# Taking hi and lo in one matmul in more weight pairs, with the MLP pairs in another order and a convolution tap on ScalarE

## The chip, the cores and the metric

The kernel runs on one core of one Trainium2 chip. The metric is the device time of one execution in microseconds; the times given are medians of several runs. The profile is of one execution, recorded by the hardware.

## The reference

One layer of a streaming encoder, sequence 512, width 1024, float32 throughout. Cut to what matters:

```python
h = rmsnorm(x, norm_mix_g)
u, v, bg, cg, xs, ga, gb = split(h @ w_in)             # seven times 1024 columns
u, v = gelu(u), rmsnorm(gelu(v), norm_v_g)
a = spatial_gating(u, v, w_s, b_s)                     # branch A
c = bg * causal_dwconv3(cg * xs, conv_w)               # branch B
m = sigmoid(ga + b) * (a @ w_proj_a) + sigmoid(gb + b) * (c @ w_proj_b)
x = x + m @ w_out
z = relu(rmsnorm(x, norm_ff_g) @ w_ff1)                # 1024 -> 4096
x = x + (z * z) @ w_ff2                                # 4096 -> 1024
return rmsnorm(x, norm_final_g)
```

`causal_dwconv3` is a convolution over time with three taps per channel.

## The kernel before, in words

Activations lie transposed: 128 channels on the partitions, 512 positions along the row. Every float32 operand is split in two fp32r parts, hi (a rounded copy, made by ScalarE, L117) and lo (what is left, a subtraction by VectorE, L118), and a product is taken as hi·hi + hi·lo + lo·hi.

Weights come in two kinds. A **unit** is one column of 128 outputs: 8 steps of depth with three matmuls of 512 columns each (`unit_k`, L265 to L267), 24 in all; two units arrive in one load of 1 MB. A **pair** is two such columns done by a fast block scheme with seven products instead of eight (P1, P2, E, P6, F, P7, D), again one load of 1 MB. For a pair VectorE also forms sums of the weight blocks (`add1`, L218; `add2`, L222 and L223); its four operands a1, s31, s42 and a22 are then split into hi and lo. Each product has four steps of depth on 256 positions. In the **narrow** form (`block_pair`, `product` with L295 to L297) each step is three matmuls of 256 columns: hi·hi, hi·lo, lo·hi, all summed in the same 256 columns of a PSUM bank. In the **wide** form (`wide_pair`, L290 and L292) the moving operand holds hi and lo side by side, so one matmul of 512 columns makes hi·hi in one half of the bank and hi·lo in the other, and one of 256 columns adds lo·hi to the first half. The two halves must then be added when the bank is emptied: ScalarE copies (L345, L351, L353, L363, L370), VectorE adds (L347, L356, L364) and folds the halves (L342, L371). The narrow form empties with half as wide copies (L311, L316, L318, L326) and additions (L313, L321, L327). P7 and D of a pair are put off (`late`): they run inside the next pair or the next unit.

Before the change the eight gate pairs are wide; the four pairs of stream c, the four of stream xs, and the sixteen of the MLP are narrow.

Operands are prepared ahead. The plan (`plan_units`, `plan_pair`) lists all loads, sums and splits in the order of use, and each unit's half and each product takes one step of it (`pump`), if one of four weight buffers is free (a22 has one of its own). A raw load is issued two loads ahead, when the splits of the load two before it have been issued, into one of two raw buffers. Work tiles of 512 (`temp`, L107) come from a pool of eight. A scheduler then lays the instructions of each engine out in its order.

Branch B (`c_pair`, four times): a pair of c, a pair of xs, two units; c is multiplied by R squared (L656, L660, L661), the product of both streams passes three taps (`conv`, first tap L668, the others L670) and a product with R (L671), and is multiplied by the units' results (L695).

The MLP: 16 pairs make 32 tiles of z (`ff1_pair`; relu times the norm's factor at L771, L776 and L777, the square at L767, the split at L117 and L118), in four chunks of eight tiles; after the pairs of a chunk come eight units of w_ff2 with that chunk's tiles, added to the result (L912). Pairs run one ahead of the chunk: 5 pairs, 8 units, 4 pairs, 8 units, 4 pairs, 8 units, 3 pairs, the last units. The z tiles lie in ten slots used in turn.

Of the kernel before, what the change touches and what calls it, by code (L numbers as in the profile page):

```python
# [9 lines left out]
F32R = mybir.dt.float32r  # L10
BF16 = mybir.dt.bfloat16
AF = mybir.ActivationFunctionType
ALU = mybir.AluOpType

P = 128
S = 512
D = 1024
KT = D // P
KS = KT // 2
NB = S // P  # L20
N2 = S // 2
HALF = 512
FT = 32
NCH = 4
CF = FT // NCH
NP1 = FT // 2
EPS = 1e-6
N_WARM = 10
N_SLOTS = 32
N_WBUF = 4  # L30


V_BGATE, V_GV, V_CONV, V_GFF, V_GFIN, V_GMIX, V_N = 0, 16, 24, 48, 56, 64, 72
# [3 lines left out]
def hybrid_block(ctx, tc, xT, vecs, w_v, w_main, w_pair, w_s, b_s, out_a, out_b):  # L37
# [12 lines left out]
    nc = tc.nc  # L50
# [46 lines left out]
    def slots(n, name, dtype=F32):  # L97
        return [Slot(f"{name}{k}", dtype) for k in range(n)]
# [8 lines left out]
    def temp(name, n=S):  # L107
        t = work.tile([P, S + 2], F32, tag="temp", name=name)
        return t[:, :n]

    def col(base, j):
        return vec[:, base + j : base + j + 1]
# [12 lines left out]
    def bank():  # L125
        return ps.tile([P, S], F32, name="bank")
# [7 lines left out]
    loads = []  # L134
    wfree = list(range(N_WBUF))
    a22_busy = [False]
# [34 lines left out]
    def add_step(fn):  # L171
        steps.append((fn, None))
# [24 lines left out]
    def plan_units(n):  # L197
        for _ in range(n // 2):
            ld = len(loads)
            loads.append(("u", len(units)))  # L200
            for e in range(2):
                units.append(add_operand(lambda ld=ld, e=e: raw_of[ld][:, 2 * e : 2 * e + 2, :]))
            add_step(lambda ld=ld: load(ld + 2))
# [3 lines left out]
    def plan_pair():  # L207
        ld = len(loads)
        loads.append(("p", len(pairs)))

        def raw(a, b):
            return raw_of[ld][:, a:b, :]

        s31, s42 = sums_t[0].t, sums_t[1].t

        def add1():

            nc.vector.tensor_tensor(s31, raw(1, 3), raw(3, 4).broadcast_to([P, 2, S]), op=ALU.add)  # L218

        def add2():  # L220

            nc.vector.tensor_tensor(s42[:, 1, :], s31[:, 1, :], raw(1, 2)[:, 0, :], op=ALU.add)  # L222
            nc.vector.tensor_tensor(s42[:, 0, :], s42[:, 1, :], raw(0, 1)[:, 0, :], op=ALU.add)  # L223

        tl = {}
        tl["a1"] = add_operand(lambda: raw(0, 2))
        add_step(add1)
        tl["s31"] = add_operand(lambda: s31)
        add_step(add2)
        tl["s42"] = add_operand(lambda: s42)  # L230
        tl["a22"] = add_operand(lambda: raw(2, 3), n=1)
        add_step(lambda: load(ld + 2))
        pairs.append(tl)
# [4 lines left out]
    def run_late():  # L238
        if late:
            late.pop(0)()  # L240
# [60 lines left out]
    def block_pair(p, right, first, second):  # L301

        A, P2, E = (bank() for _ in range(3))
        A_, P2_, E_ = (b[:, :N2] for b in (A, P2, E))
        c1, c2 = temp("c1"), temp("c2")
        product(p, right, "P1", A, True)  # L310
        nc.scalar.copy(c1[:, :N2], A_)  # L311
        product(p, right, "P2", P2, True)
        nc.vector.tensor_add(c1[:, :N2], P2_, c1[:, :N2])  # L313
        run_late()
        product(p, right, "E", E, True)
        nc.scalar.copy(c2[:, N2:], E_)  # L316
        product(p, right, "P6", A, False)
        nc.scalar.copy(c1[:, N2:], A_)  # L318
        run_late()
        product(p, right, "F", E, False)  # L320
        nc.vector.tensor_add(c1[:, N2:], E_, c1[:, N2:])  # L321
        first(c1)

        def p7():
            product(p, right, "P7", A, False)
            nc.scalar.copy(c2[:, :N2], A_)  # L326
            nc.vector.tensor_add(c2[:, N2:], c2[:, :N2], c2[:, N2:])  # L327

        def dd():
            product(p, right, "D", A, False)  # L330
            second(A_, c2)

        late.extend([p7, dd])
# [97 lines left out]
            nc.vector.tensor_add(acc, acc, sq)  # L431


    sums_t = slots(2, "wsum")
    plan_units(KT)
    for _ in range(KS):
# [9 lines left out]
    plan_units(KT)  # L446
    n_win = len(pairs)
    for ck in range(NCH):
        for _ in range(CF // 2 + (ck == 0) - (ck == NCH - 1)):
            plan_pair()  # L450
        plan_units(KT)


    xin_s = slots(KS, "xin")
# [62 lines left out]
    for i in range(2 * KT):  # L517
        h, k = divmod(i, KT)
# [36 lines left out]
    R2 = small.tile([P, S], F32, name="R2")  # L555
# [39 lines left out]
    for j in range(KT):  # L595
# [8 lines left out]
    right_x = right_of(  # L604
        lambda sl: x_s[sl].t[:, :, :N2], x_s[KS:], xc1, xc2
    )
# [17 lines left out]
    def next_pair():  # L624
        pair_no["next"] += 1
        return pair_no["next"] - 1
# [25 lines left out]
    def c_pair(j0):  # L652
        tc_, ys = {}, {}

        def c_first(c1):
            nc.vector.tensor_mul(c1, c1, R2)  # L656
            tc_[0] = c1

        def c_second(n21, c2):
            nc.vector.tensor_mul(c2[:, :N2], n21, R2[:, :N2])  # L660
            nc.vector.tensor_mul(c2[:, N2:], c2[:, N2:], R2[:, N2:])  # L661
            tc_[1] = c2

        def conv(e, z):
            j = j0 + e
            y = temp("y")
            w = [col(V_CONV + 8 * i, j) for i in range(3)]
            nc.vector.tensor_scalar(y, z[:, 0:S], w[0], None, op0=ALU.mult)  # L668
            for i in (1, 2):
                nc.vector.scalar_tensor_tensor(y, z[:, i : S + i], w[i], y, op0=ALU.mult, op1=ALU.add)  # L670
            nc.vector.tensor_mul(y, y, R)  # L671
            ys[e] = y

        def x_first(c1):
            z = temp("z", S + 2)
            nc.vector.memset(z[:, 0:2], 0.0)
            nc.vector.tensor_mul(z[:, 2 : S + 2], tc_[0], c1)
            conv(0, z)

        def x_second(n21, c2):  # L680

            z = temp("z", S + 2)
            nc.vector.memset(z[:, 0:2], 0.0)
            nc.vector.tensor_mul(z[:, 2 : N2 + 2], n21, tc_[1][:, :N2])
            nc.vector.tensor_mul(z[:, N2 + 2 : S + 2], c2[:, N2:], tc_[1][:, N2:])
            conv(1, z)

        block_pair(next_pair(), right_x, c_first, c_second)
        block_pair(next_pair(), right_x, x_first, x_second)
        pbs = []  # L690
        for e in range(2):
            pbs.append(bank())
            unit_matmuls(pbs[e], xh, xl)
        for e in range(2):
            nc.vector.tensor_mul(ys[e], pbs[e], ys[e])  # L695
            split_into(ch[j0 + e], cl[j0 + e], ys[e])
# [13 lines left out]
    for p in range(KS):  # L710
        gate(next_pair(), 1, 2 * p, sgs.__setitem__)
        last = p == KS - 1
        for e in range(2):
            j = 2 * p + e
# [25 lines left out]
    right_f = right_of(f_b11, fb2, ft1, ft2)  # L740
    xg = {}
    for n in range(KT):
        j = n // 2 + KS * (n % 2)
# [13 lines left out]

    acc2 = None
    Rf = small.tile([P, S], F32, name="R")
    z_s = slots(CF + 2, "z", F32R)  # L760

    def z_tile(i):
        t = z_s[i % len(z_s)].t
        return t[:, 0, :], t[:, 1, :]

    def z_split(i, t):
        nc.scalar.activation(t, t, AF.Square)  # L767
        split_into(*z_tile(i), t)
# [2 lines left out]
        nc.vector.scalar_tensor_tensor(c1, c1, 0.0, Rf, op0=ALU.max, op1=ALU.mult)  # L771
        z_split(i, c1)

    def z_second(i, n21, c2):

        nc.vector.scalar_tensor_tensor(c2[:, :N2], n21, 0.0, Rf[:, :N2], op0=ALU.min, op1=ALU.mult)  # L776
        nc.vector.scalar_tensor_tensor(c2[:, N2:], c2[:, N2:], 0.0, Rf[:, N2:], op0=ALU.min, op1=ALU.mult)  # L777
        z_split(i, c2)
# [77 lines left out]
    def ff1_pair(p):  # L856
        def first(c1):
            if p == 0:
                wait_rf.append(lambda: z_first(0, c1))
            else:  # L860
                z_first(2 * p, c1)

        def second(n21, c2):
            z_second(2 * p + 1, n21, c2)

        block_pair(n_win + p, right_f, first, second)
        if p == 0:
            r2.append(rstd_of(acc))

            def p7_and_rf(p7=late.pop(0)):  # L870
                p7()
                nc.vector.tensor_copy(Rf, spread(r2[0]))
                wait_rf.pop()()
            late.insert(0, p7_and_rf)
# [17 lines left out]
            release(us[e])  # L892
        return dict(enumerate(pys))

    done = 0
    for ck in range(NCH):
        end = min((ck + 1) * CF // 2 + 1, NP1)
        for p in range(done, end):
            ff1_pair(p)
        done = end  # L900
        zh, zl = zip(*[z_tile(ck * CF + i) for i in range(CF)])
        last = ck == NCH - 1
        if last:
            acc2 = [acc[:, :256], acc[:, 256:]]
        pys = side_by_side(zh, zl) if last else {}
        for j in range(KT - 2 if last else KT):
            if j in pys:
                py = pys[j]
            else:
                py = bank()  # L910
                unit_matmuls(py, zh, zl)
            nc.vector.tensor_add(res[j], py, res[j])  # L912
            if last:
                for hf in range(2):
                    sum_squares(acc2[hf], res[j][:, hf * N2 : (hf + 1) * N2], j, n=N2)
                scale_g(j, slice(0, S))
        if last:
            give(*fb11, *fb2, *ft1, *ft2)
            last_tiles([KT - 2, KT - 1])
# [67 lines left out]
```

## Time and profile before

| | us |
|---|---|
| median of 3 runs | 787.3 (786.64 to 787.36) |
| the profiled execution | 786.65 |
| its span, first to last instruction | 784.9 |
| TensorE busy | 776.3 |
| VectorE busy | 584.5 |
| ScalarE busy | 373.6 |

The profile lists, for each engine, when its instructions ran. PE is TensorE's matmuls, PEld its weight loads, DVE is VectorE, ACT ScalarE, SP the queue that issues the loads. A matmul's recorded length runs past the start of the next one, so the pace of matmuls is read from start to start. VectorE's and ScalarE's records overlap a little in the same way when an engine does not wait.

### The profile page before, as it was taken

To read this page: it belongs to the slowest core of one execution; us is meant where nothing else is said; L and a number is where in the kernel's file an instruction comes from. 1 tells how busy PE (TensorE), PEld (TensorE's weight loads), DVE (VectorE), ACT (ScalarE), POOL (GpSimd) and SP (SyncE) were. 2 spreads that over 40 slices of the span, in tenths; PEclk is the share of its full clock that TensorE was granted. 3 is DMA by queue.
4 is the path that set the end of the run, shared out by engine and by line. 5 is a ranking of instruction groups with operands and counts; after the bars stand their busy time and mean duration, and the time that the engine had idled before them with its cause. 6 is when DMAs were issued, how large, how long until landed. Compare 5 with 4: busy or idle time off the path is not lost.

```text
span 784.9 us, 11159 instructions
## 1 busy us (share of the span) xinstructions
PE 776.3 (99%) x4574; PEld 689.4 (88%) x4574; DVE 584.5 (74%) x878; ACT 373.6 (48%) x556; POOL 6.3 (1%) x14
## 2 busy tenths in 40 slices
PE   9999999999999999999999999999999999999996
PEld 6888888889999998888888999889988999889886
DVE  7849787777889889877779997647855686557644
ACT  8625364444344354544556576315642465226421
POOL 0000000000000000000000000000000000000000
PEclk9999999999999999999999999999999999999999
DMA  9602113331332223332633034320353024311403
GB/s 337 218 38 92 69 55 108 108 108 55 112 123 89 108 75 142 108 107 102 220 108 107 1 109 144 125 107 1 109 193 129 1 98 171 108 55 54 161 1 108
DMA packets 21442, 83.59 MB, mean 106 GB/s; under 512 B 1936, under 2 KB 2960, under 8 KB 17296
## 3 DMA queue, kind: packets, MB, share of 16 engines
q1 hardware_dynamic: 20384, 81.27, 29.5%
q10 hardware_dynamic: 1008, 1.61, 0.6%
q8 instruction: 36, 0.59, 0.3%
q14 instruction: 14, 0.11, 0.0%
HBM read 80.78 MB, written 2.10 MB: 106 GB/s over the span
## 4 chain that ended last, share of the span: by engine, by line
PE 96%; DMA 1%; DVE 1%; ACT 1%; issue 0%; POOLq 0%; DVEq 0%
PE bank L265 17%; PE bank L266 17%; PE bank L267 17%; PE bank L297 10%; PE bank L296 10%; PE bank L295 10%; PE bank L290 7%; PE bank L530 6%; PE bank L292 3%; PE bank L581 1%; DMA raw<-w_pair 1%; DVE wlo L118 0%; DMA vec<-vecs 0%; PE bank L422 0%; ACT whi L117 0%
## 5 line engine op out<-in xcount | busy, mean ns | idle before, releaser
L117 ACT CAST whi<-raw 128x1024 fp32r<-128x1024 f32 (+1 forms) x136 | 129.0, 950 | 160.8 <-PE bank L266 111.0
L118 DVE TENSOR_TENSOR wlo<-raw,whi 128x1024 fp32r<-128x1024 f32 (+1 forms) x136 | 148.7, 1094 | 17.0 <-ACT whi L117 15.4
L265 PE MATMUL bank<-z,whi 128*128 128x512 f32 (+1 forms) x272 | 102.7, 378 | 0.0
L266 PE MATMUL bank<-z,whi 128*128 128x512 f32 (+1 forms) x272 | 102.5, 377 | 0.0
L267 PE MATMUL bank<-z,wlo 128*128 128x512 f32 (+1 forms) x272 | 102.4, 376 | 0.0
L117 ACT CAST whi<-wsum 128x1024 fp32r<-128x1024 f32 x64 | 67.2, 1050 | 69.5 <-PE bank L266 39.0
L118 DVE TENSOR_TENSOR wlo<-wsum,whi 128x1024 fp32r<-128x1024 f32 x64 | 78.1, 1220 | 11.1 <-ACT whi L117 10.9
L297 PE MATMUL bank<-ft,wlo 128*128 128x256 f32 x256 | 72.5, 283 | 0.6 <-DVE wlo L118 0.6
L295 PE MATMUL bank<-ft,whi 128*128 128x256 f32 x256 | 72.5, 283 | 0.0
L296 PE MATMUL bank<-ft,whi 128*128 128x256 f32 x256 | 72.4, 283 | 0.0
L912 DVE TENSOR_TENSOR res<-bank,res 128x512 f32<-128x512 f32 x30 | 20.7, 691 | 60.4 <-PE bank L267 60.4
L267 PEld LDWEIGHTS bank<-z,wlo 128*128 128x128 f32 x272 | 51.2, 188 | 9.4
L265 PEld LDWEIGHTS bank<-z,whi 128*128 128x128 f32 x272 | 51.2, 188 | 9.1
L266 PEld LDWEIGHTS bank<-z,whi 128*128 128x128 f32 x272 | 51.2, 188 | 8.9
L296 PE MATMUL bank<-fb,whi 128*128 128x256 f32 x192 | 54.4, 283 | 0.0
L295 PE MATMUL bank<-fb,whi 128*128 128x256 f32 x192 | 54.4, 283 | 0.0
L297 PE MATMUL bank<-fb,wlo 128*128 128x256 f32 x192 | 54.3, 283 | 0.0
L265 PE MATMUL bank<-x,whi 128*128 128x512 f32 x128 | 50.4, 394 | 0.0
L266 PE MATMUL bank<-x,whi 128*128 128x512 f32 x128 | 50.0, 390 | 0.0
L267 PE MATMUL bank<-x,wlo 128*128 128x512 f32 x128 | 49.8, 389 | 0.0
L297 PEld LDWEIGHTS bank<-ft,wlo 128*128 128x128 f32 x256 | 49.1, 192 | 0.8 <-DVE wlo L118 0.8
L295 PEld LDWEIGHTS bank<-ft,whi 128*128 128x128 f32 x256 | 49.1, 192 | 0.3
(174 smaller groups left out, 1755.4 us busy)
## 6 DMA issues: line engine op xcount, KB each, us to landing
raw<-w_main SPq DMA_DIRECT2D x36, 1024.0 KB, 5.0
raw<-w_pair SPq DMA_DIRECT2D x32, 1024.0 KB, 4.8
vraw<-w_v SPq DMA_DIRECT2D x16, 256.0 KB, 5.4
xin<-xT SPq DMA_DIRECT2D x8, 256.0 KB, 5.0
res<-xT SPq DMA_DIRECT2D x8, 256.0 KB, 4.1
out_a<-o SPq DMA_DIRECT2D x4, 256.0 KB, 2.3
wsT<-w_sT ACTq DMA_DIRECT2D x2, 256.0 KB, 4.7
bsb<-b_sb ACTq DMA_DIRECT2D x2, 256.0 KB, 6.6
```

The source lines that it names most:

```text
L117: nc.scalar.copy(hi, src)
L118: nc.vector.tensor_tensor(lo, src, hi.bitcast(F32), op=ALU.subtract)
L265: nc.tensor.matmul(psum, hi[:, c], act_hi[k][:, cols], start=k == 0, stop=False)
L266: nc.tensor.matmul(psum, hi[:, c], act_lo[k][:, cols], start=False, stop=False)
L267: nc.tensor.matmul(psum, lo[:, c], act_hi[k][:, cols], start=False, stop=k == KT - 1)
L290: nc.tensor.matmul(two, w_hi[sl], x2[sl], start=first and sl == 0, stop=False, **kw)
L292: nc.tensor.matmul(half, w_lo[sl], x2[sl][:, 0, :], start=False, stop=sl == KS - 1, **kw)
L295: nc.tensor.matmul(half, w_hi[sl], x2[sl][:, 0, :], start=first and sl == 0, stop=False, **kw)
L296: nc.tensor.matmul(half, w_hi[sl], x2[sl][:, 1, :], start=False, stop=False, **kw)
L297: nc.tensor.matmul(half, w_lo[sl], x2[sl][:, 0, :], start=False, stop=sl == KS - 1, **kw)
L530: nc.tensor.matmul(vbanks[h][b], xs[k][:, b * P : (b + 1) * P], ws, start=k == 0 and ws is vh and xs is xh, stop=k == KT - 1 and xs is xl,)
L912: nc.vector.tensor_add(res[j], py, res[j])
```

## The change

Eleven MLP pairs (all but the first five) and the four pairs of stream c take the wide form. The order of the MLP is now, in each chunk, first a group of pairs, then four units, then one pair, then four units: 5 pairs (narrow), 4 units, 1 pair, 4 units; 3 pairs, 4 units, 1 pair, 4 units; the same once more; 2 pairs and the last units. The plan of loads follows the same order. Tiles of z lie in twelve slots instead of ten. The first tap of the convolution is a scaled copy on ScalarE. `c_second` and `z_second` work on a whole row of 512 instead of two halves; for the narrow MLP pairs the old form is kept as `z_second_ps`.

```diff
+N_NARROW = 5
+    def ff1_parts(ck):
+        h = CF // 2
+        ends = [min(ck * h + h + e, NP1) for e in (1, 2)]
+        begin = min(ck * h + 2, NP1) if ck else 0
+        return [range(begin, ends[0]), range(ends[0], ends[1])]
 ...
     for ck in range(NCH):
-        for _ in range(CF // 2 + (ck == 0) - (ck == NCH - 1)):
-            plan_pair()
-        plan_units(KT)
+        for part in ff1_parts(ck):
+            for _ in part:
+                plan_pair()
+            plan_units(KT // 2)
 ...
-        def c_second(n21, c2):
-            nc.vector.tensor_mul(c2[:, :N2], n21, R2[:, :N2])
-            nc.vector.tensor_mul(c2[:, N2:], c2[:, N2:], R2[:, N2:])
+        def c_second(c2):
+            nc.vector.tensor_mul(c2, c2, R2)
             tc_[1] = c2
 ...
-            nc.vector.tensor_scalar(y, z[:, 0:S], w[0], None, op0=ALU.mult)
+            nc.scalar.activation(y, z[:, 0:S], AF.Copy, scale=w[0])
 ...
-        block_pair(next_pair(), right_x, c_first, c_second)
+        wide_pair(next_pair(), right_x, c_first, c_second)
         block_pair(next_pair(), right_x, x_first, x_second)
 ...
-    z_s = slots(CF + 2, "z", F32R)
+    z_s = slots(CF + 4, "z", F32R)
 ...
+    def z_second(i, c2):
+        nc.vector.scalar_tensor_tensor(c2, c2, 0.0, Rf, op0=ALU.min, op1=ALU.mult)
+        z_split(i, c2)
 ...
-        block_pair(n_win + p, right_f, first, second)
+        if p < N_NARROW:
+            block_pair(n_win + p, right_f, first, lambda n21, c2: z_second_ps(2 * p + 1, n21, c2))
+        else:
+            wide_pair(n_win + p, right_f, first, second)
 ...
     for ck in range(NCH):
-        end = min((ck + 1) * CF // 2 + 1, NP1)
-        for p in range(done, end):
+        parts = ff1_parts(ck)
+        for p in parts[0]:
             ff1_pair(p)
 ...
         for j in range(KT - 2 if last else KT):
+            if j == KT // 2:
+                for p in parts[1]:
+                    ff1_pair(p)
```

## Rows read from the trace of the kernel before

**Rows 1.** Busy us, share of the span and instructions of two engines, the page.
```profile
PE 776.3 (99%) x4574; PEld 689.4 (88%) x4574; DVE 584.5 (74%) x878; ACT 373.6 (48%) x556; POOL 6.3 (1%) x14
```
**Rows 2.** Waits of TensorE: waiter, releaser, us in total, times, longest.
```profile
PE bank L297 <- DVE wlo L118: 0.6, 1, 0.6
```
**Rows 3.** Chain that ended last, in time order: start us, length us, what.
```profile
548.51 6.52 DMA raw<-w_pair
```
**Rows 4.** Busy us by stretch: span, PE, PEld, DVE, ACT, POOL, clock, DMA share, GB/s.
```profile
185.67:309.10 123.43, 123.43 (x858) 115.66 (x857) 106.55 (x162) 52.48 (x79) 0.00 (x0) 1.00 0.27 95
436.00:484.80 48.80, 48.80 (x409) 48.77 (x409) 45.01 (x73) 33.53 (x56) 1.91 (x1) 1.00 0.20 66
532.20:572.00 39.80, 39.25 (x318) 38.59 (x317) 31.95 (x47) 23.86 (x41) 0.00 (x0) 1.00 0.20 65
```
**Rows 5.** Timeline of TensorE, narrow MLP products: start us, length us, instruction.
```profile
473.24 0.28 PE L295 MATMUL bank<-fb,whi 128*128 128x256 f32 x1
...
477.56 0.28 PE L295 MATMUL bank<-ft,whi 128*128 128x256 f32 x1
```
**Rows 6.** Timeline of TensorE, two wide products of a gate pair.
```profile
100.39 1.09 PE L290 MATMUL bank<-x,whi 128*128 128x512 f32 x4
101.32 0.63 PE L292 MATMUL bank<-x,wlo 128*128 128x256 f32 x4
101.79 1.09 PE L290 MATMUL bank<-xc,whi 128*128 128x512 f32 x4
```
**Rows 7.** Chain in time order, first product of two successive gate steps.
```profile
350.56 0.91 PE bank L290 x4
...
371.28 0.91 PE bank L290 x4
```
**Rows 8.** Timeline of VectorE: two steps of branch B, two MLP units.
```profile
203.23 0.49 DVE L668 TENSOR_SCALAR y<-z,vec 128x512 f32<-128x512 f32 x1
...
234.33 0.49 DVE L668 TENSOR_SCALAR y<-z,vec 128x512 f32<-128x512 f32 x1
...
515.11 0.69 DVE L912 TENSOR_TENSOR res<-bank,res 128x512 f32<-128x512 f32 x1 [3.36 <-PE bank L267]
...
520.55 0.69 DVE L912 TENSOR_TENSOR res<-bank,res 128x512 f32<-128x512 f32 x1 [3.35 <-PE bank L267]
```
**Rows 9.** Timeline of VectorE, back to back in the run of four pairs.
```profile
542.56 1.21 DVE L118 TENSOR_TENSOR wlo<-raw,whi 128x1024 fp32r<-128x1024 f32 x1
543.69 0.68 DVE L223 TENSOR_TENSOR wsum<-wsum,raw 128x512 f32<-128x512 f32 x1
544.29 0.41 DVE L327 TENSOR_TENSOR c<-c 128x256 f32<-128x256 f32 x1
544.62 1.22 DVE L118 TENSOR_TENSOR wlo<-wsum,whi 128x1024 fp32r<-128x1024 f32 x1
```
**Rows 10.** Instruction groups by shape: count, busy us, mean ns, idle before.
```profile
L347 DVE TENSOR_TENSOR t<-bank,t 128x512 f32<-128x512 f32 x8 | 5.5, 685 | 0.5 <-PE bank L292 0.5
L345 ACT COPY t<-bank 128x512 f32<-128x512 f32 x8 | 4.7, 586 | 4.2 <-PE bank L292 4.2
L668 DVE TENSOR_SCALAR y<-z,vec 128x512 f32<-128x512 f32 x8 | 3.9, 482 | 0.1
L748 ACT ACTIVATE xg<-res,vec 128x512 f32<-128x512 f32 x8 | 5.8, 722 | 1.9 <-DVE res L746 1.7
```
**Rows 11.** Timeline of VectorE, run of four: first and last of three waits, the fetch.
```profile
534.37 0.42 DVE L313 TENSOR_TENSOR c<-bank,c 128x256 f32<-128x256 f32 x1 [0.86 <-PE bank L297]
...
538.69 0.42 DVE L321 TENSOR_TENSOR c<-bank,c 128x256 f32<-128x256 f32 x1 [0.90 <-PE bank L297]
...
555.05 1.22 DVE L218 TENSOR_TENSOR wsum<-raw 128x1024 f32<-128x1024 f32 x1 [2.38 <-DMA raw<-w_pair]
```
**Rows 12.** Loads on SP's queue, the page: count, KB each, median us to landing.
```profile
raw<-w_main SPq DMA_DIRECT2D x36, 1024.0 KB, 5.0
```
**Rows 13.** Timeline, last MLP pair: VectorE's last lo part, TensorE's matmul that reads it.
```profile
735.65 0.69 DVE L118 TENSOR_TENSOR z<-c,z 128x512 fp32r<-128x512 f32 x1 [1.35 <-ACT z L117]
...
738.95 0.39 PE L265 MATMUL bank<-z,whi 128*128 128x512 f32 x1
```

More of the change, by code (lines that the diff above doesn't have):

```diff
@@ L772, in z_first, with z_second_ps @@
         z_split(i, c1)
-    def z_second(i, n21, c2):
+    def z_second(i, c2):
+        nc.vector.scalar_tensor_tensor(c2, c2, 0.0, Rf, op0=ALU.min, op1=ALU.mult)
+        z_split(i, c2)
+    def z_second_ps(i, n21, c2):
         nc.vector.scalar_tensor_tensor(c2[:, :N2], n21, 0.0, Rf[:, :N2], op0=ALU.min, op1=ALU.mult)
@@ L861, in first, with second @@
                 z_first(2 * p, c1)
-        def second(n21, c2):
-            z_second(2 * p + 1, n21, c2)
-        block_pair(n_win + p, right_f, first, second)
+        def second(c2):
+            z_second(2 * p + 1, c2)
+        if p < N_NARROW:
+            block_pair(n_win + p, right_f, first, lambda n21, c2: z_second_ps(2 * p + 1, n21, c2))
+        else:
+            wide_pair(n_win + p, right_f, first, second)
         if p == 0:
@@ L893, in side_by_side @@
         return dict(enumerate(pys))
-    done = 0
     for ck in range(NCH):
-        end = min((ck + 1) * CF // 2 + 1, NP1)
-        for p in range(done, end):
+        parts = ff1_parts(ck)
+        for p in parts[0]:
             ff1_pair(p)
-        done = end
         zh, zl = zip(*[z_tile(ck * CF + i) for i in range(CF)])
```

## The prediction, made before the change was run

> **What bounds the kernel now.** I read the busy times first: TensorE works in 776.3 of 784.9 us, one matmul per weight load [rows 1]. A busy TensorE proves little by itself, so the list of its waits came next: in the whole span it waited once for another engine in mid-kernel, 0.6 us for a lo operand of VectorE [rows 2]. The chain in order of time shows where: between 548 and 565 us, in the run of four MLP pairs of the second chunk, behind a transfer of a pair's weights of 6.52 us [rows 3]. Then the stretches: in branch B (185.67 to 309.10) VectorE is busy 106.55 of 123.43 us; in the run of the first five MLP pairs 45.01 of 48.80; in the run of four, 31.95 of 39.80 [rows 4]. So TensorE's pace sets the end, and VectorE is the next bound, with little room where narrow pairs stand back to back. The reader should keep both in mind: the change buys TensorE time with VectorE time.
>
> **What TensorE gains.** A narrow product is 12 matmuls of 256 columns, a wide one 4 of 512 and 4 of 256: the same 3072 columns. Three narrow products (36 matmuls) start at 473.24 and the next at 477.56: 4.32 / 3 = 1.44 us [rows 5]. Wide products of the gate pairs start at 100.39 and 101.79: 1.40 us, 0.93 for the four wide matmuls and 0.47 for the four half ones [rows 6]. So a product gives 0.04 us and a pair of seven 0.28. A second way checks it: a gate step (one wide pair, two units) repeats every 371.28 - 350.56 = 20.72 us [rows 7], a unit every 520.55 - 515.11 = 5.44 us, and a step of branch B (two narrow pairs, two units) every 234.33 - 203.23 = 31.10 us [rows 8]. That makes a wide pair 20.72 - 10.88 = 9.84 and a narrow one (31.10 - 10.88) / 2 = 10.11: 0.27 us. Pairs made wide: 11 of the MLP's 16 and the 4 of c, 15 in all: **15 x 0.28 = 4.2 us off**.
>
> The Trainium skill ("TensorE: Matmul & The Clock Gate", section "Wait — 56ns, not 53.3ns?") speaks against this: it has a matmul take its columns at 2.4 GHz plus about 2.5 ns, so that four matmuls fewer per product would give an estimated 0.01 us instead of 0.04, and 1 us in all instead of 4.2. The rows do not agree: 256 columns are spaced 0.12 us in the narrow product and 0.1175 in the wide one, 512 columns 0.2325.
>
> **What VectorE pays.** Back to back, its instructions are spaced 1.13 us (128x1024), 0.60 (128x512) and 0.33 (128x256), less than their recorded lengths [rows 9]. I count by these. Preparing a pair's weights: three 1024 differences, one 1024 sum, one 512 difference, two 512 sums: 4 x 1.13 + 3 x 0.60 = 6.3 us, unchanged. Narrow emptying: three 256 additions, 1.0. Wide emptying: three 512 additions and four of 256: 3.1. An addition of 512 that reads the accumulator (0.685 us recorded) is as long as one of 512 elsewhere, so the same spacings serve [rows 9, 10]. The MLP's own work on the two results: 2.5 narrow, 2.4 wide. So an MLP pair needs 9.8 us of VectorE narrow and **11.8 wide, against TensorE's 9.8**: each wide pair in a run loses 2 us of VectorE's lead.
>
> ScalarE gains four copies of 0.59 in place of four of half the width and one half copy, under 1.3 us more per pair; it is busy 23.86 of 39.80 us in the run of four [rows 4], so I cost it at nothing while it does not wait.
>
> **Branch B.** Per step the c pair adds 2.1 us to VectorE (the two R2 products become one). The first tap leaves it: 2 x 0.48 us recorded [rows 10], 0.8 by spacing. Net +1.3, and TensorE's step is 0.28 shorter. VectorE's idle time there is (123.43 - 106.55) / 4 = 4.2 us a step, so 2.6 us remain. Both taps cost ScalarE 0.72 each [rows 10] and it is busy only 52.48 of 123.43 us. The new wait (VectorE's second tap behind ScalarE's first) has queued behind it the pair's own last two taps and the lo differences of coming operands; these are several us early. I take nothing; the bounds are 0 and 0.7 us a step (one tap fully exposed), 2.9 in all.
>
> **The MLP order.** Before, runs of 5, 4, 4 and 3 pairs; after, 5 narrow, then 4 units, 1 wide, 4 units; twice 3 wide, 4 units, 1 wide, 4 units; 2 wide and the last units. A single pair sits among units where VectorE works about 1.7 of each 5.44 us: covered. The run of four with the 0.6 us stall is gone: **-0.6**. The question is the run of three. At its start the first pair's operands are ready and the second's sums too. By the time TensorE needs the third pair's s42 (16 products, 22.4 us later) VectorE must have done: emptying and results of the first pair 5.5, operands of the second 4.0, of the third up to s42 5.7, emptying of the second and the first piece of the third 4.9: 20.1 us. Before, three early waits for TensorE between 534 and 539 us took 2.27 us of such a run whatever the load [rows 11]. 20.1 + 2.3 = 22.4: just enough, nothing left. Then the first unit behind the run: its raw weights can be fetched only when the second pair's a22 is split, some 17 us into the run; the fetch takes 5.0 us as a median and 6.52 in the run of before [rows 3, 12]; copy and difference add 2.3 us. That is 24.3 to 25.8 against a need at 26.6. Each of the two runs may stall between 0 and 2.5 us (1.5 if the chain waits of the run of before come on top, 1.0 if the fetch meets a queue). I take 0.5, near the low end, since the sum just closes: **+1.0**. SP's queue holds the loads in the new order, two ahead as before; the single pair's load goes between two unit loads, each with more than 5 us to spare.
>
> **The end.** The last pair's second result passes one more ScalarE copy and one more addition, about 1 us. Before, its lo part started at 735.65 and the unit that reads it at 738.95 [rows 13]: 2.6 us of slack cover it. Nothing.
>
> **Sum.** The profiled execution took 786.65 us (span 784.9, 1.75 around it), 0.65 below the median of 787.3. 786.65 - 4.2 - 0.6 + 1.0 = 782.85, so -3.8; for the median 787.3 - 3.8 = **783.5 us**.
>
> **The rivals.**
> 1. *VectorE eats it up.* The stalls of the runs reach 2.5 us each and branch B some tenths: 787.3 - 4.8 + 3.5 to 6 = 786 to 788.5. For it: a VectorE without room in the run. Against: before lost only 0.6 us in a run of four in which 2.38 us of VectorE went to one fetch [rows 11]. Chance 0.15.
> 2. *Columns alone set the pace*, 0.227 us per 512 as in a steady unit (5.44 / 24), halves in proportion: then narrow and wide products cost the same, and the time is 787.3 - 0.6 + 1.0 = 787.7. The rule of the Trainium skill weighed above lies near this, by its estimate 1 us lower. Against: the two measured pairs, 9.84 and 10.11. Chance 0.03.
> 3. *Slower: the work tiles lock the run.* Eight tiles are shared. A wide pair opens five at its start while the pair before still holds three (both results and one sum); the sixth, for P7, must wait for a fold. If VectorE is over about 1.5 us late there, ScalarE's copy stands in its queue with the next hi copies behind it, VectorE waits for these, and the lead is lost: the five wide pairs that follow another in a run then go at VectorE's 11.8, not 9.8, 5 x 2.0 = 10 us: 787.3 - 4.8 + 10 = 792.5. For it: eight tiles fully used. Against: my sum leaves VectorE late by tenths, not 1.5. Chance 0.08.
>
> **How the numbers follow.** The forecast has 0.74. About 0.2% (1.6 us) is what a measurement of this kernel can tell from no change. Faster (under 785.7): 0.74. Same: rivals 1 and 2, 0.18. Slower: rival 3, 0.08. The low end has no stall: 787.3 - 4.8, and 0.3 for the spread of the runs: 782.2. The high end takes in both stalls at 2.5: 787.3 - 4.8 + 5.0 = 787.5; I stop at 787.2, which leaves out under 2 in 10.
>
> **What would show it.** Right: c and MLP products of the sixth pair on at 1.40 us; branch B's step at 30.8; TensorE's waits under 2 us in all, and those at the third pair of a run or the unit behind it; VectorE above 9 tenths in the runs of three. Wrong: products at 1.44 (rival 2), TensorE waiting for emptying additions or ScalarE copies in runs (rival 3), waits in branch B behind the first tap.

## The result, and the profile after

The changed kernel takes 782.3 us as a median (782.0 to 782.8), the kernel before 787.0 in the runs taken with it (786.6 to 787.4). The ratio is 0.994, with a 95% interval of 0.9927 to 0.9952: 4.7 us less (by the interval 3.8 to 5.7), where 3.8 were predicted. The profiled execution took 782.3 us, with a span of 780.5.

The page after, busy times by engine:

```profile
PE 772.9 (99%) x4154; PEld 667.1 (85%) x4154; DVE 608.2 (78%) x915; ACT 393.6 (50%) x579; POOL 6.3 (1%) x14
```

Beside [rows 1], TensorE has 420 matmuls less: 15 wide pairs x 7 products x 4 matmuls. It is busy 3.4 us less, VectorE 23.7 us more. The 0.6 us wait of [rows 2] is not in the list; the only wait of TensorE that the list shows is at the start of the kernel:

```profile
PE st L79 <- DVE warm L66: 1.0, 1, 1.0
```

The chain that ended last runs almost wholly through TensorE: where [rows 3] had a transfer in it, the page now has

```profile
PE 98%; DMA 0%; ACT 0%; DVE 0%; POOLq 0%; DVEq 0%; issue 0%
```

The timeline of TensorE, products of an MLP pair in the second chunk, and those of the first c pair (columns: start, length, instruction):

```profile
559.94 1.09 PE L291 MATMUL bank<-ft,whi 128*128 128x512 f32 x4
560.87 0.64 PE L293 MATMUL bank<-ft,wlo 128*128 128x256 f32 x4
561.34 1.09 PE L291 MATMUL bank<-ft,whi 128*128 128x512 f32 x4
...
562.74 1.09 PE L291 MATMUL bank<-ft,whi 128*128 128x512 f32 x4
...
185.00 1.07 PE L291 MATMUL bank<-x,whi 128*128 128x512 f32 x4
...
186.38 1.09 PE L291 MATMUL bank<-x,whi 128*128 128x512 f32 x4
```

From 559.94 to 561.34 to 562.74, and from 185.00 to 186.38, it is 1.38 to 1.40 us a product, the pace of [rows 6], where the narrow ones took 1.44 [rows 5]. Two steps of branch B, on VectorE, now start 233.83 - 203.04 = 30.79 us apart, against 31.10 in [rows 8]:

```profile
203.04 0.69 DVE L685 TENSOR_TENSOR z<-c,c 128x512 f32<-128x512 f32 x1
...
233.83 0.69 DVE L685 TENSOR_TENSOR z<-c,c 128x512 f32<-128x512 f32 x1
```

Busy times by stretch (span, PE, PEld, DVE, ACT, POOL, clock, DMA share, GB/s): branch B, the first run of three wide pairs, and the run of five narrow ones. They answer [rows 4].

```profile
184.99:308.10 123.11, 123.11 (x753) 110.54 (x752) 110.22 (x167) 62.06 (x91) 0.00 (x0) 1.00 0.29 99
540.10:566.70 26.60, 26.60 (x151) 23.07 (x150) 23.26 (x33) 18.06 (x27) 0.00 (x0) 1.00 0.13 41
436.00:484.00 48.00, 48.00 (x403) 47.98 (x402) 44.46 (x72) 32.76 (x56) 1.91 (x1) 1.00 0.19 67
```

TensorE is busy in the whole of each. VectorE is idle for 12.9 of 123.11 us in branch B, 3.2 a step, and works 23.26 of 26.60 us, 87%, in the first run of three; the prediction had named more than nine tenths as a sign.

**Where the time went.** I added up, over the two traces, the distance from each matmul's start to the next one's, by the kind of matmul that begins it:

| us | products of pairs | units | first stage (V) | span |
|---|---|---|---|---|
| before | 320.9 (2240 of 256 columns, 224 of 512) | 394.4 | 43.8 | 784.9 |
| after | 315.8 (1400 and 644) | 394.7 | 44.2 | 780.5 |

The products give 5.15 us; 0.71 of that is the one long gap of before (0.83 us in place of 0.12), the other 4.44 are pace, 0.30 for each of the 15 pairs. Units and the first stage, whose work the change doesn't touch, took 0.3 and 0.35 us more, all other matmuls 0.1 more.

### The profile page after: what moved, and what is told of

It is laid out like the page before. It is cut to its first block, busy times and chain, and to the rows that moved or that the text cites. A ratio compares the mean times of both kernels' runs of the same rounds, so it can differ in the third digit from the quotient of the medians.

```text
span 780.5 us, 10415 instructions
## 1 busy us (share of the span) xinstructions
PE 772.9 (99%) x4154; PEld 667.1 (85%) x4154; DVE 608.2 (78%) x915; ACT 393.6 (50%) x579; POOL 6.3 (1%) x14
## 4 chain that ended last, share of the span: by engine, by line
PE 98%; DMA 0%; ACT 0%; DVE 0%; POOLq 0%; DVEq 0%; issue 0%
PE bank L291 19%; PE bank L266 17%; PE bank L267 17%; PE bank L268 17%; PE bank L293 10%; PE bank L539 6%; PE bank L296 4%; PE bank L297 4%; PE bank L298 4%; PE bank L590 1%; DMA vec<-vecs 0%; PE bank L423 0%; PE st L412 0%; PE bank L811 0%; PE st L857 0%; DVE ob L823 0%
## 5 line engine op out<-in xcount | busy, mean ns | idle before, releaser
L291 PE MATMUL bank<-xc,whi 128*128 128x512 f32 x192 | 52.2, 393 | 0.0
L266 PE MATMUL bank<-x,whi 128*128 128x512 f32 x128 | 50.4, 394 | 0.0
L267 PE MATMUL bank<-x,whi 128*128 128x512 f32 x128 | 50.0, 390 | 0.0
L291 PE MATMUL bank<-ft,whi 128*128 128x512 f32 x176 | 47.8, 393 | 0.0
L539 PE MATMUL bank<-vp,x 128*128 128x512 f32 x192 | 44.5, 392 | 0.1
L539 PEld LDWEIGHTS bank<-vp,x 128*128 128x128 f32 x192 | 36.1, 189 | 8.5 <-ACT vp L118 1.0
L219 DVE TENSOR_TENSOR wsum<-raw 128x1024 f32<-128x1024 f32 x32 | 39.0, 1220 | 3.6 <-DMA raw<-w_pair 3.4
L291 PE MATMUL bank<-x,whi 128*128 128x512 f32 x144 | 39.2, 394 | 0.0
L291 PEld LDWEIGHTS bank<-xc,whi 128*128 128x128 f32 x192 | 33.9, 189 | 5.4
L775 ACT ACTIVATE c<-c 128x512 f32<-128x512 f32 x32 | 20.2, 632 | 30.9 <-DVE c L784 16.2
```

The costliest lines, as they stand in the source:

```text
L266: nc.tensor.matmul(psum, hi[:, c], act_hi[k][:, cols], start=k == 0, stop=False)
L267: nc.tensor.matmul(psum, hi[:, c], act_lo[k][:, cols], start=False, stop=False)
L291: nc.tensor.matmul(two, w_hi[sl], x2[sl], start=first and sl == 0, stop=False, **kw)
L539: nc.tensor.matmul(vbanks[h][b], xs[k][:, b * P : (b + 1) * P], ws, start=k == 0 and ws is vh and xs is xh, stop=k == KT - 1 and xs is xl,)
```

## The experiments

**One half of the change each: branch B, and the MLP.** The first kernel is the one before with its c pairs wide and the first tap on ScalarE; the second is the changed one with both undone.

Against the kernel before:

```diff
-        def c_second(n21, c2):
-            nc.vector.tensor_mul(c2[:, :N2], n21, R2[:, :N2])
-            nc.vector.tensor_mul(c2[:, N2:], c2[:, N2:], R2[:, N2:])
+        def c_second(c2):
+            nc.vector.tensor_mul(c2, c2, R2)
 ...
-            nc.vector.tensor_scalar(y, z[:, 0:S], w[0], None, op0=ALU.mult)
+            nc.scalar.activation(y, z[:, 0:S], AF.Copy, scale=w[0])
 ...
-        block_pair(next_pair(), right_x, c_first, c_second)
+        wide_pair(next_pair(), right_x, c_first, c_second)
```

> The kernel before with only branch B changed: the four c pairs wide, the first tap on ScalarE; the MLP is untouched. Theory (each wide pair gives TensorE 0.28 us, VectorE's extra work fits in its idle time): 4 x 0.28 = 1.1 us off, 787.0 to 785.9; branch B's step goes from 31.10 to 30.8 us, no wait of TensorE in branch B, the 0.6 us wait in the run of four MLP pairs stays. Rival (columns alone set TensorE's pace): no gain, step 31.1 us. Rival (VectorE or the tap's new wait holds TensorE up): waits of TensorE in branch B, up to 0.7 us a step, time 786 to 789.

> The changed kernel with branch B as before: c pairs narrow, first tap on VectorE; the MLP has its wide pairs and its new order. Theory: 11 x 0.28 = 3.1 us off for the wide pairs and 0.6 for the run of four that is gone: 783.3. Columns alone: 0.6 off at most, 786.4. With the first experiment the two gains should add up to the whole change's 4.7 us.

Branch B alone took 785.5 us against 786.7 for the kernel before, ratio 0.9988 (0.9974 to 1.0003); the MLP alone 783.6, ratio 0.9965 (0.9951 to 0.9978). The differences, 1.2 and 3.1 us, add up to 4.3, and the whole change gave 4.7; but the interval of the first takes in no gain at all. The distances of the starts say more: the products take 1.74 us less than before in the first kernel and 3.81 in the second. Without the one long gap of before (0.71) that is 1.03 for four pairs and 3.10 for eleven, 0.26 and 0.28 a pair. TensorE's waits in the first kernel beyond the first stage come to 0.2 us, in a gate step, so nothing waits behind the first tap.

One expectation failed: the 0.6 us wait was to stay in the first kernel, whose MLP is that of before, and it is not there. The sum that had waited 2.38 us for a fetch of 6.52 us [rows 3, 11] now waits for one of 4.72 us:

```profile
553.12 1.22 DVE L218 TENSOR_TENSOR wsum<-raw 128x1024 f32<-128x1024 f32 x1 [0.58 <-DMA raw<-w_pair]
```

So the wait goes with one slow fetch in the profiled execution of before. The old order runs without it.

**The order without the wide form.** All MLP pairs narrow, in the new order, twelve slots for z (excerpt):

```diff
+N_NARROW = NP1
 ...
+        for part in ff1_parts(ck):
+            for _ in part:
+                plan_pair()
+            plan_units(KT // 2)
 ...
-    z_s = slots(CF + 2, "z", F32R)
+    z_s = slots(CF + 4, "z", F32R)
```

> The new order of MLP pairs and units alone, with twelve z tiles, every MLP and c pair narrow, the first tap on VectorE. Theory: only the one wait of 0.6 us goes: 786.4, products still 1.44 us apart. Rival (the order and the relief of VectorE, not the wide matmuls, make the gain): 783 to 784.

786.6 us, ratio 0.9998 (0.9989 to 1.0006). The 0.6 us wait is gone; beside the one at the start of the kernel, the list of TensorE's waits has only this, in the first stage:

```profile
PE bank L539 <- ACT vp L118: 0.2, 1, 0.2
```

In this trace the products' sum is 0.88 us shorter than before, 0.71 of it the long gap, and units and first stage are 0.25 and 0.5 us longer. A gain of 0.6 lies within the interval of the time, and so does none: by itself the order isn't worth anything that can be measured. The kernel with the MLP's half has the same order and slots and differs from this one by its eleven wide pairs alone: 783.6 against 786.6 us, 3.0 us or 0.27 a pair. VectorE is busy 605.1 us there against 584.9 here, 1.84 a wide pair.

**The wide form without the order.** Eleven wide pairs and the wide c stream as after, in the runs of before (5, 4, 4 and 3 pairs, each followed by eight units):

```diff
-        ends = [min(ck * h + h + e, NP1) for e in (1, 2)]
-        begin = min(ck * h + 2, NP1) if ck else 0
-        return [range(begin, ends[0]), range(ends[0], ends[1])]
+        end = min(ck * h + h + 1, NP1)
+        return [range(ck * h + 1 if ck else 0, end), range(end, end)]
```

> The changed kernel with the old order of the MLP: 5 pairs, 8 units, twice 4 pairs and 8 units, 3 pairs and the last units; wide from the sixth pair on, c wide, tap on ScalarE. By my sum a run of three wide pairs just closes, and each further wide pair costs VectorE 2 us more than TensorE, so the two runs of four should stall 1 to 3 us each: 784.5 to 788. If VectorE still has lead to spare in a run of four: 782.5 to 783, no waits of TensorE. If the eight work tiles lock a run once VectorE is late: waits of TensorE of 2 us per pair, over 788.

783.7 us (783.7 to 784.0), ratio 0.9958 (0.9945 to 0.9971): 1.4 us slower than the changed kernel. TensorE's waits, and the chain of waits around the first of them (start, length, what):

```profile
PE bank L291 <- ACT t L352: 0.9, 2, 0.5
```

```profile
557.95 0.61 DVE wlo L119
...
558.57 4.95 DMA raw<-w_main
...
563.55 1.05 ACT whi L118
564.60 0.53 ACT c L774
565.13 0.51 ACT whi L118
565.64 0.52 ACT z L118
566.16 0.49 ACT t L352
...
566.69 1.20 PE bank L291 x4
```

At the end of each run of four, TensorE waits for a bank that ScalarE has yet to copy (L352): product F goes on in the bank of product E, when E's result has been copied. That copy stands in ScalarE's queue behind the hi copy of a unit whose weights landed only at 563.52, because VectorE's difference before it (557.95) came late, and behind three more. So the order is worth something, but only for wide pairs. Two causes were left: the fetch of the unit's weights (4.95 us), and VectorE's work.

**The fetch made shorter.** The same kernel, with each load of two units cut in two of 512 KB:

```diff
-            nc.sync.dma_start(
-                r.rearrange("p (u a) s -> p u (a s)", u=2), w_main[i : i + 2].rearrange("u p f -> p u f")
-            )
+            for e in range(2):
+                nc.sync.dma_start(r[:, 2 * e : 2 * e + 2, :].rearrange("p a s -> p (a s)"), w_main[i + e])
```

> The kernel of the old order (5, 4, 4, 3 pairs, wide from the sixth) with each load of two units cut in two loads of half a megabyte, so that the first unit's raw weights land earlier. In that kernel TensorE stood in both runs of four behind ScalarE's copy of E, which stood behind the hi copy of the first unit's weights, which waited for a fetch of 4.95 us. Theory (the late fetch, through ScalarE's queue, is the stall): the fetch of the first half takes 2.5 to 4 us, the two waits go or fall under 0.3 us, 783.7 to 782.3. Rival (VectorE's work is the stall, the fetch only coincides): 783.7 stays.

784.9 us, ratio 0.9977 (0.9968 to 0.9986): 1.2 us slower than with whole loads. The fetch is out of the chain, and the wait is still there (L351 is the copy that was L352):

```profile
565.86 0.92 PE bank L290 x4
...
566.81 0.62 ACT whi L118
...
567.95 0.49 ACT t L351
...
568.48 1.19 PE bank L290 x4
```

```profile
PE bank L290 <- ACT t L351: 0.6, 2, 0.3
...
PE bank L265 <- ACT z L118: 0.3, 1, 0.3
PE bank L290 <- ACT t L363: 0.3, 1, 0.3
```

The first half load lands 3.3 us after its issue, so the fetch was shortened as meant. But ahead of E's copy there now stands a hi copy (566.81) that waits for a product of TensorE itself (565.86), and the kernel gained new waits elsewhere. One wait took the place of another, so this kernel doesn't say how much of the 0.9 us was the fetch's. What the waits have in common is that E's copy stands in ScalarE's queue behind other work.

**VectorE's work made less.** The run-of-four kernel again, without the first weight sum of the pairs from the seventh on, 1.13 us of VectorE each:

```diff
-        add_step(add1)
+        if len(pairs) < 4 * KS + 6:
+            add_step(add1)
```

> The kernel of the old order (runs of 5, 4, 4, 3 pairs, wide from the sixth) with VectorE's first weight sum (1.14 us) left out for the MLP pairs from the seventh on: those pairs multiply with the sum of an earlier pair. Nothing else is taken from any engine. Theory (VectorE's work is what makes the two runs of four late): 3 x 1.14 = 3.4 us less in each run, the two waits of TensorE behind ScalarE's copy of E go, 783.7 to 782.4. Rival (the fetch and ScalarE's queue alone make the wait): both waits stay, 783.7.

782.8 us (782.2 to 784.2), ratio 0.9951 (0.9939 to 0.9963), 0.9 less than with the sum, and as fast as the changed kernel within the spread. The traced execution is the slowest of the five, 784.2 us. The waits for L352 (here L353) are gone; in the middle of the kernel 0.3 us are left:

```profile
PE bank L292 <- ACT t L365: 0.3, 1, 0.3
```

The fetch is as long as before (5.0 us), so VectorE's work decides whether the runs of four wait. How it does so shows at the end of the run in the second chunk. E's copy and F in the changed kernel, with the old order, and without the sum:

```profile
566.26 0.58 ACT L352 COPY t<-bank 128x512 f32<-128x512 f32 x1
567.62 1.07 PE L291 MATMUL bank<-fb,whi 128*128 128x512 f32 x4
...
566.06 0.58 ACT L352 COPY t<-bank 128x512 f32<-128x512 f32 x1
566.69 1.20 PE L291 MATMUL bank<-fb,whi 128*128 128x512 f32 x4 [0.40 <-ACT t L352]
...
567.88 0.58 ACT L353 COPY t<-bank 128x512 f32<-128x512 f32 x1
569.02 1.07 PE L292 MATMUL bank<-fb,whi 128*128 128x512 f32 x4
```

| | E starts | its copy, us later | matmuls of the next unit ahead of F | that unit's first lo part done | F waits |
|---|---|---|---|---|---|
| changed kernel | 561.34 | 4.92 | 9 | 564.6 | no |
| old order | 561.48 | 4.58 | 2 | 568.2 | 0.40 |
| old order, half loads | 562.91 | 4.94 | 4 | 569.9 | 0.31 |
| old order, without the sum | 563.20 | 4.68 | 7 | 567.6 | no |

E's copy comes no earlier where nothing waits. What differs is how much TensorE has to do before F. With the old order VectorE makes the unit's lo part only after F has begun, with whole loads and with halves, and the scheduler laid just two or four of the unit's matmuls, which need no lo part of the weights, in front of F. Without the sum the lo part is ready in time for seven. So VectorE's lateness seems to cost TensorE the work that would have covered E's copy. This is read from the traces: taking the sum away also changed the order of TensorE's instructions, and no run kept the order and changed VectorE's time alone.

**VectorE's work made more, where the pairs stand after the change.** The changed kernel, with four more passes of VectorE over each wide MLP pair's results, 4 x 0.33 us by spacing (the operand is multiplied by 1.0; excerpt):

```diff
+            def more(c):
+                for _ in range(2):
+                    nc.vector.tensor_scalar(c, c, 1.0, None, op0=ALU.mult)
```

> The changed kernel with four further VectorE passes in each wide MLP pair, multiplications by one, two on each result: 4 x 0.40 = 1.6 us more per pair. By the sum of the prediction a run of three is just full, with 2.4 us more of VectorE's work before the third pair's s42: waits of about 2 us in each of the two runs, 786 to 787. Rival (results may come late without TensorE waiting, so the run has lead to spare): no waits or under 0.5 us each, 782.3 to 783.2.

782.9 us (782.4 to 783.3), ratio 0.9951 (0.9939 to 0.9962). TensorE doesn't wait in the runs of three, and is as busy there as in the changed kernel:

```profile
540.10:566.70 26.60, 26.60 (x152) 23.19 (x151) 23.75 (x39) 18.01 (x26) 0.00 (x0) 1.00 0.12 41
```

VectorE is busy 621.9 us in the whole span against 608.2, 1.25 more for each of the eleven pairs, but only 0.5 more in this stretch: other work of it moves behind the run, where units give it room. Little of that slack is left, though. The third pair's last operand is ready 4.4 us later in its run than in the changed kernel (next section):

```profile
564.01 1.22 DVE L119 TENSOR_TENSOR wlo<-wsum,whi 128x1024 fp32r<-128x1024 f32 x1
```

It is done at 565.2, and TensorE's first matmul with a lo part behind the start of that product (563.32) is at 565.18: the scheduler laid eight matmuls of 512 columns in a row ahead of it, where the changed kernel has four. So a run of three bears 1.25 us more of VectorE a pair, with TensorE's order adapted to it.

**More wide pairs: all of them, 13 of the 16, and the xs stream.**

```diff
-N_NARROW = 5
+N_NARROW = 0
```

With 3 in place of 0 it is thirteen. For the xs stream (excerpt):

```diff
-            nc.vector.tensor_mul(z[:, 2 : N2 + 2], n21, tc_[1][:, :N2])
-            nc.vector.tensor_mul(z[:, N2 + 2 : S + 2], c2[:, N2:], tc_[1][:, N2:])
+            nc.vector.tensor_mul(z[:, 2 : S + 2], c2, tc_[1])
 ...
-        block_pair(next_pair(), right_x, x_first, x_second)
+        wide_pair(next_pair(), right_x, x_first, x_second)
```

> The changed kernel with the first five MLP pairs wide too, so a run of five wide pairs without a unit between. TensorE's pace gives 5 x 0.28 = 1.4 us. VectorE: the run of five is busy 44.46 of 48.0 us narrow; wide it needs 5 x 2.06 = 10.3 us more and has 1.4 us less time, 8.2 us short against some 3 us of lead at its end. Theory (VectorE's work bounds a run once the lead is used up): waits of 3 to 6 us in this run, net 784 to 787 against the changed kernel's 782.3. Rival (a run is only hurt by late fetches, and VectorE's results may be late without TensorE waiting): 780.9 to 782.

> The changed kernel with only the first three MLP pairs narrow: the run of five ends in two wide pairs. TensorE's pace gives 2 x 0.28 = 0.56 us: 781.7 if VectorE still has lead there. The run of five is busy on VectorE 44.46 of 48.0 us; two wide pairs add 4.1 us, 0.6 more than its idle time with the shorter span, against some 3 us of lead at its end: I expect 781.8. If its idle time cannot be filled: waits of 1 us or more, 782.5 to 784.

> The changed kernel with the xs pairs of branch B wide as well. TensorE's pace gives 4 x 0.28 = 1.1 us. VectorE works 2.05 us more per step; of its 3.2 us idle 0.9 would remain in a step of 30.5 us. Theory (sums decide, the rest waits for itself): 781.2, step of 30.5 us. Rival (with VectorE above 0.96 of a step its waits no longer fit and TensorE waits): step stays at 30.8 or longer, 782.3 to 785.

All wide: 788.5 us (786.1 to 791.4), ratio 1.002 (1.0007 to 1.0034), slower than the kernel before. In the profiled execution (786.3 us) TensorE waits, and the chain shows VectorE working without a break:

```profile
PE bank L291 <- ACT whi L118: 3.1, 2, 1.7
```

```profile
453.41 0.69 DVE wlo L119
454.11 0.60 DVE z L119
454.71 0.60 DVE c L784
...
457.44 0.61 DVE c L779
```

```profile
436.00:485.00 49.00, 45.41 (x254) 38.25 (x253) 47.05 (x77) 34.02 (x53) 1.85 (x1) 1.00 0.18 65
```

In the stretch of five wide pairs VectorE is busy 47.05 of 49.00 us and TensorE only 45.41. Here VectorE is the bound: the first rival's mechanism, in the place where the change leaves the pairs narrow. The executions of this kernel differ by 5 us, and the profiled one is among the shortest, so the trace shows only part of its loss.

Thirteen wide: 782.7 us (781.6 to 785.3), ratio 0.9952 (0.9937 to 0.9966), not to be told from the changed kernel's 782.3. The 0.56 us that the pace of two more pairs should bring doesn't show in the trace either: the products take 316.0 us against 315.8. TensorE waits 0.3 us for a hi copy in the run of five; the rest of what is missing stays open.

The xs stream wide as well: 784.4 us (784.0 to 784.6), ratio 0.997 (0.9958 to 0.9982), 2.1 us slower than the changed kernel, where the sum made it 1.1 us faster. Busy times of branch B:

```profile
185.80:309.00 123.20, 121.96 (x636) 103.01 (x635) 113.72 (x173) 65.24 (x94) 0.00 (x0) 1.00 0.27 97
```

VectorE is busy 92% of the stretch, 2.4 us idle a step, and yet TensorE is idle for 1.24 us there, most of it before 224.1 and 294.3; it loses 0.25 us more behind the stage, at 314.5. So an average of 92% does not close. The likely reason, read from the chain and not tested, is that the work comes in clusters (two pairs' emptying, then the taps); the chain of the first loss also begins with a fetch of 6.09 us.

**The first tap back on VectorE.** The changed kernel with this alone undone:

```diff
-            nc.scalar.activation(y, z[:, 0:S], AF.Copy, scale=w[0])
+            nc.vector.tensor_scalar(y, z[:, 0:S], w[0], None, op0=ALU.mult)
```

> The changed kernel with the first tap back on VectorE, everything else as changed. VectorE then works 0.8 us more per step of branch B, where it has 3.2 us idle. Theory: nothing changes, 782.3, no waits of TensorE in branch B. Rival (the wide c pair needs the relief): waits of 0.5 us or more a step, 784 or more.

782.3 us (782.1 to 782.8), ratio 0.9945 (0.9933 to 0.9957), and no wait of TensorE in branch B. The move of the tap is worth nothing here: branch B has room for the wide c pair without it.

## Why the prediction was right, and where it was off

The time came out 0.1 us above the low end of the range (782.2 to 787.2), the end that has no stall in it. The mechanism was right; two of the smaller terms were not, and their errors, 0.6 one way and 1.0 the other, partly cancel. That the gain was missed by no more than 0.9 us is partly luck. What the runs support is 4.4 us, from the pace alone; the 0.3 beyond it lies within the interval.

**The pace of the products: right.** 0.28 us a pair was predicted; the traces give 0.30 for the whole change, 0.26 and 0.28 for its halves. The term of -4.2 measured -4.4. The second rival is out: with columns alone the eleven wide pairs would not have brought 3.0 us at the same order. In the products of the changed kernel 512 columns took 0.231 us on average and 256 columns 0.119. The rule of the Trainium skill ("TensorE: Matmul & The Clock Gate", section "Wait — 56ns, not 53.3ns?") makes it 0.216 and an estimated 0.109, and by it the estimate was 1 us for all 15 pairs. It doesn't hold for these matmuls: fewer of them for the same columns are worth about four times what it gives.

**The wait of 0.6 us: not a cost of the order.** It is gone after the change, 0.71 us by the distances of the starts. But it is gone as well in the kernel with branch B's half, which has the old order, and the order alone left the time the same within its interval. The prediction took a wait that one slow fetch made in one execution for a property of the run of four.

**The stalls in the runs of three, +1.0: mis-sized; they measured 0.** The prediction added up all that VectorE does between the run's start and the third pair's s42, 20.1 us, with 2.3 us of early waits on top, and set it against 22.4. But what it put in front of s42 need not all come before it. VectorE's timeline, just before and in the first run of three:

```profile
537.88 0.69 DVE L224 TENSOR_TENSOR wsum<-wsum,raw 128x512 f32<-128x512 f32 x1
...
558.37 0.68 DVE L357 TENSOR_TENSOR t<-bank,t 128x512 f32<-128x512 f32 x1
558.97 1.22 DVE L119 TENSOR_TENSOR wlo<-wsum,whi 128x1024 fp32r<-128x1024 f32 x1
...
560.44 0.68 DVE L119 TENSOR_TENSOR z<-c,z 128x512 fp32r<-128x512 f32 x1
...
561.64 0.68 DVE L348 TENSOR_TENSOR t<-bank,t 128x512 f32<-128x512 f32 x1
562.36 0.42 DVE L343 TENSOR_TENSOR c<-t 128x256 f32<-128x256 f32 x1
563.37 1.23 DVE L119 TENSOR_TENSOR wlo<-raw,whi 128x1024 fp32r<-128x1024 f32 x1 [0.58 <-ACT whi L118]
```

The third pair's s42 (558.97) is done at 560.2, 2.5 us before its product starts at 562.74. The start was as assumed (the second pair's sums are ready at 538.6), and so were the early waits, 2.35 us. Counted by spacing, VectorE does 16.2 us of the listed work from the start to the end of that operand, not 20.1. Behind it come the split of the first pair's second result (560.44, 0.6 us) and 3.3 us of the emptying: most of the second pair's and the third's first piece (561.64, 562.36). The unit behind the run came much as predicted: its weights' fetch is issued 16.8 us into the run ("some 17"), and its first lo part is done at 564.6, 24.5 us into the run ("24.3 to 25.8"); TensorE first uses it at 566.01, a little before the 26.6 of the prediction.

What the prediction doesn't have at all is that the scheduler may lay matmuls of the next unit between the last products of a run. In the changed kernel nine stand ahead of the third pair's F, and cover the copy that F needs.

**How near the edge it was.** The mechanism of that step is real one pair further on: runs of four wide pairs wait 0.9 us in all, a run of five in the middle of 436 to 485 us makes VectorE the bound. The 2 us of VectorE that a wide pair takes was about right: 1.84 measured.

**Branch B at nothing: right.** The step is 30.79 us (30.8 predicted) and VectorE's idle time 3.2 us a step (2.6 predicted). The tap's move was not what made room; without it there is no wait either. What did not hold, when carried on to the xs stream, is the way of counting: idle time left over on the average of a step was taken as enough.

**ScalarE at nothing "while it does not wait": right after the change, and the condition is what counts.** TensorE does not wait for it beyond the list shown above. In the runs of four the list names ScalarE: a hi copy that waited 0.66 us for weights stands ahead of the copy that frees TensorE's bank. Yet that copy comes no later behind its product than in the changed kernel; TensorE has less to do meanwhile. The third rival had this the other way round, a copy that waits for a work tile with hi copies behind it, and a lead lost for good; the runs of four lost 0.9 us in two waits, not 10, and recovered. Whether the eight work tiles have a part in it no run here tells; more of them were not tried.

**The end at nothing: right.** TensorE doesn't wait in the last pairs.

## What to carry to other kernels

Where TensorE sets the end and each of its matmuls costs something beside its columns, as it does here, joining two operands into one wider matmul pays, and the pay can be read beforehand from two products of either form in the same trace. The price lies on the engines that empty the accumulators, and is to be summed over a run of such work, not over a stage: a single wide pair among plain units was free, three in a row were, four cost 0.5 us a run, and with five VectorE set the pace. In such a sum, count ahead of an operand only what must come ahead of it, since a scheduler may put results behind. And before a wait is put down to the order of the work, look for it in a second trace: a single slow fetch can make one.

## What the runs showed of the hardware that was not expected

The first stage, which no kernel here changed, is not always equally long: 50.0 us of matmuls in the traced execution of the kernel with the MLP's half alone (789.7 us, its median 783.6), 43.8 before. TensorE waits there 4.3 us for ScalarE. Behind this wait the clock granted is 0.74 of 2.4 GHz from 36 to 42 us, as part of that stretch is at the level of 1.2 GHz:

```profile
36.00:42.00 6.00, 6.00 (x21) 4.86 (x20) 6.00 (x18) 5.44 (x10) 0.00 (x0) 0.74 0.06 25
```

The chain that leads to the wait comes from loads of the start:

```profile
23.54 5.49 DMA vraw<-w_v
...
33.45 1.33 POOL r L405
34.80 0.70 ACT vt L502
35.55 0.65 PE bank L539
```

In the changed kernel the last loads of `vraw` are issued by 21.6 us, here at 23.5 and later. Why the loads are late in some executions stays open. Two executions of the kernel with branch B's half alone took 789.2 us, the others 784.7 to 785.7; whether for the same reason, no trace tells.

Cutting a load in two brings its first half sooner and the whole hardly: of the 72 loads of 512 KB, issued in twos, the first of two landed in 3.4 us as a median and the second in 4.3, counted from its own issue some 0.4 us later; the 36 of 1 MB took 4.9.
